# Modulation sets, squares and roots, and low parts of branch weights in a two-layer diffusion trunk

## The chip, the cores and the metric

The kernel runs on one core of one Trainium2 chip. The metric is the device time of one execution in microseconds (us). A core has five engines with their own instruction streams: TensorE (PE, matrix products, written to PSUM), VectorE (DVE), ScalarE (ACT), GpSimd (POOL) and SyncE (SP), which issues the loads and stores. SBUF is the working memory, and PSUM holds eight banks of 512 float32 columns. An engine waits on semaphores that other engines or transfers raise, and works its own list strictly in order.

## The reference, cut to what matters

Two sequences go through two layers with the same weights: 512 latent tokens and 128 context tokens. The kernel keeps them side by side as 640 columns.

```python
def trunk_layer(x, cvec, lp, mix_fn):
    sh1, sc1, g1, sh2, sc2, g2 = modulation(cvec, lp['w_mod'], lp['b_mod'])
    mixed, kv = mix_fn(rmsnorm(x, lp['norm1_g']) * (1.0 + sc1) + sh1)
    x = x + g1 * mixed
    x = x + g2 * swiglu(rmsnorm(x, lp['norm2_g']) * (1.0 + sc2) + sh2, lp['w_ffn_in'], lp['w_ffn_out'])
    return x, kv

def merge_branches(out_a, out_b, out_c, gates, lp, lam_init):
    ...
    ga, gb, gc = jnp.split(jax.nn.sigmoid(gates), N_BRANCH, axis=-1)
    return (ga * ya + gb * yb + gc * yc) @ lp['w_out']

def modulation(cvec, w_mod, b_mod):
    m = jax.nn.silu(cvec) @ w_mod + b_mod
    return [t[:, None, :] for t in jnp.split(m, N_MOD, axis=-1)]

def rmsnorm(x, g):
    y = xf * lax.rsqrt(jnp.mean(xf * xf, axis=-1, keepdims=True) + EPS)
    return (y * g.astype(jnp.float32)).astype(x.dtype)
```

`D_MODEL` is 1024, the FFN is 2816 wide, and everything is float32. After the second layer there is one more `rmsnorm`.

## The kernel before

**Products.** Activations lie as eight tiles of 128 channels by 640 tokens. A product in float32 is made of three in a faster format: weight and activation are each split into a high part and a low part, and `group` (L486) issues high x high (L491), high x low (L492) and low x high (L493) over a half of 320 tokens. Weights come in chunks of 128x1024, 512 KB each, through `weights` (L386): SP loads `raw` (two buffers), ACT copies it to `whi`, rounding it, and the low part `wlo` is raw minus whi. There are four buffers of each. The low part is made in one of two ways. Normally POOL subtracts (`ptt`, L375). For chunks with the flag `add`, which are the input projection, the gates and the branch projections from the tenth chunk on, ACT writes minus raw, rounded, into `wlo`, and POOL issues a transfer that adds raw to it in the DMA engines (`dma_add`, L380). After L0's branch C come the chunks of the output projection, and they are POOL's again.

**A layer.** Attention with its three branches; then `gate_tile` (L1460) for branch C, the merge: for each of eight channel tiles a gate product (one chunk) and a branch product (half a chunk), tanh on ACT, and on DVE `th` times the branch, added to `acc` and split into `u`. Then `out_proj` (L1523): eight tiles times two halves of tokens, 24 matmuls each; DVE adds the residual (`residual`, L1515) from the bank, ACT squares the result (`square_add`, L702), DVE adds the square to `ssq`, and the bank was given back before the square. `rstd` (L712) sums `ssq` over the channels with a product by ones (L717), and ACT and DVE make the reciprocal root; `norm` (L731) then makes the high and low parts of h per tile: DVE multiplies x by a column and by the root, ACT adds the shift, and DVE, or POOL for tiles 2 and 5, makes the low part. Then the FFN in three parts of 8, 8 and 6 tiles (`PARTS`): `ffn_in`, whose tiles from the fourth on use seven half products in place of eight (`seven`, L1638), with sums of weights made on DVE into `ws` and `raw2` (`sums` in `weights`), and sums of h made on DVE into `act` and `ht` (`seven_inputs`, L1607); then `ffn_out` (L1729), whose last part ends with the residual, the squares and the next norm.

**Modulation.** A layer has 24 sets of 256 outputs: sets 0 to 7 for shift and scale of norm 1, 8 to 11 the first gate, 12 to 19 shift and scale of norm 2, 20 to 23 the second gate. They are computed on DVE while PE works (`mod_dve`, L565): SP loads a 128x512 piece `mr` of the transposed weight (four buffers), DVE multiplies it by the vector of one of the two sequences and sums the row (L617). A set takes eight such instructions, and then a few of 128x4 (`mod_finish`, L683). The vectors lie in the PSUM tiles named S at a merge and in banks named B (tag T) in an FFN. Layer 0's sets 0 to 7 are done at the start; its sets 8 to 19 during layer 0's merge and `out_proj`; its sets 20 to 23 and layer 1's sets 0 to 19 during layer 0's FFN; and layer 1's sets 20 to 23 during layer 1's FFN.

**What sets the order.** Every engine's list is fixed when the program is built. `_Order` is a small planner: tasks (generators) with priorities offer their next instruction to an engine with an assumed cost, and the engine takes the one that is ready with the lowest number. Dense products have 1000, modulation 200, the norms about 8. Four PSUM banks are shared by the tags D (up to four) and T (up to two), four more hold the scores S and later the tag F; the FFN uses six of them in turn.

Of the kernel before, what the change touches and what calls it, by code (L numbers as in the profile page):

```python
# [27 lines left out]
ALU = mybir.AluOpType  # L28
# [54 lines left out]
MOD_SOON, MOD_SPREAD = 0.7, 0.75  # L83

ADD_FROM = 10
ENGINES = ("PE", "ACT", "DVE", "POOL", "SP")

# [170 lines left out]
class _Trunk:  # L258
# [127 lines left out]
    def weights(self, plan):  # L386
# [6 lines left out]
        for i, (l, src) in enumerate(plan):  # L393
            seven = isinstance(src, tuple)
            n = 4 if seven else 1
            c = {"l": l, "src": src, "seven": seven, "add": i >= ADD_FROM and not seven and src < O_WO, "hi_ok": [self.ev() for _ in range(n)],
                 "lo_ok": [self.ev() for _ in range(n)]}
            for e in ("loaded", "loaded2", "s1", "s3", "s4"):
                c[e] = self.ev()
            todo.append(c)  # L400
# [164 lines left out]
    def mod_dve(self, steps, prio, each, home):  # L565
# [5 lines left out]
        sets = list(dict.fromkeys(s for _, ss in steps for s in ss))  # L571
        left = {s: 4 for s in sets}
        n = 512 if home == "T" else D
# [32 lines left out]
        def use():  # L606
            md = yield from self.get("md", [P, 512])
            ma = (yield from self.get("ma", [P, 8 * len(sets)])).rearrange("p (j q c s) -> p j q c s", q=2, c=2, s=2)
            for at, pieces, ok, done in plan:
                yield self.wait(ok)  # L610
                for (l, j), q, i, e, d in pieces:
                    a = ma[:, sets.index((l, j))]
                    yield self.wait(e)
                    for c in range(2):
                        o = 0 if at is not None else i * 512
                        b, r = cv[c][:, o:o + 512], a[:, q, c, i:i + 1]
                        yield ("DVE", each, lambda w=d["raw"], b=b, r=r: nc.vector.scalar_tensor_tensor(  # L617
                            md, w, 1.0, b, op0=ALU.mult, op1=ALU.mult, accum_out=r), 0.13)
                    self.rel("mr")
                    left[l, j] -= 1  # L620
                    if left[l, j] == 0:
                        yield self.tt(a[:, :, :, 0], a[:, :, :, 0], a[:, :, :, 1], ALU.add)
                        yield from self.mod_finish(l, j, a[:, :, :, 0])
                self.o.fire(done)
            for t in ("ma", "md", home, home):
                self.rel(t)
# [55 lines left out]

    def mod_finish(self, l, j, t):  # L683

        out = self.modc[l][:, 2 * j:2 * j + 2, :]
        bm = self.small[l][:, S_BM + 2 * j:S_BM + 2 * j + 2].rearrange("p (q o) -> p q o", o=1).to_broadcast([P, 2, 2])
        yield self.tt(out, t, bm, ALU.add)
        which = j // 4
        if which in (1, 4):
            k = 2 * (j % 4)  # L690
            g = (S_N1 if which == 1 else S_N2) + k
            a = self.acol[l][:, 8 * (which == 4) + k:8 * (which == 4) + k + 2, :]
            gb = self.small[l][:, g:g + 2].rearrange("p (q o) -> p q o", o=1).to_broadcast([P, 2, 2])
            yield self.stt(a, out, 1.0, gb, ALU.add, ALU.mult)
        elif which == 2:
            k = 2 * (j % 4)
            yield self.ts(self.g1h[l][:, k:k + 2, :], out, 0.5, None, ALU.mult)
        self.o.fire(self.mod_ok[l][j])

    def square_add(self, x, half, ssq, first):  # L702
        s = slice(half * HALF, (half + 1) * HALF)
        if first:
            yield self.act(ssq, x[:, s], AF.Square)
        else:
            q = yield from self.get("sq", [P, HALF])
            yield self.act(q, x[:, s], AF.Square)
            yield self.tt(ssq, ssq, q, ALU.add)
            self.rel("sq")  # L710

    def rstd(self, ssq):  # L712

# [15 lines left out]
        return ssq  # L729

    def norm(self, l, which, x, half, ssq, h, ready, done):  # L731

        r = yield from self.rstd(ssq)
        left = [KT]

        def one(kt):
# [26 lines left out]
            if left[0] == 0:  # L763
                self.rel("ssq")
                self.o.fire(done)

# [756 lines left out]
    def out_proj(self, l, order, x2, ssq, ssq_ok):  # L1523
# [16 lines left out]
        for m, half in order:  # L1540
# [188 lines left out]
    def ffn_out(self, l, part, act, act_ok, x, ssq, ssq_ok, save):  # L1729
# [6 lines left out]
        def after(m, half, d):  # L1736
            yield self.wait(self.mod_ok[l][20 + m // 2])
            xh = x[m][:, half * HALF:(half + 1) * HALF]
            yield from self.residual(x[m], xh, d, half, self.modc[l][:, 40 + m, :])
            self.bank_done(d)  # L1740
            if not end:
                return
            if m == half == 0:
                self.o.spawn(self.preload(), 8)
            yield from self.square_add(x[m], half, ssq[half], m == 0)
            hits[half]()
# [35 lines left out]
    def layer(self, l, h, norm1, close):  # L1782
# [79 lines left out]
        def control():  # L1862
# [25 lines left out]
            yield self.wait(out_done)  # L1888
            if l == 0:
                for j in range(8, 20):  # L1890
                    yield self.wait(self.mod_ok[l][j])
                mctx.close()
            octx.close()
# [7 lines left out]
            no.close()  # L1901
            mctx = self.pool("m", mods)
            here, ahead = [(l, j) for j in range(20, 24)], [(l + 1, j) for j in range(20)]
            steps = [((0,), here), ((1,), here)]
            if not last:
                steps += [((1,), ahead), ((0,), ahead)]
            self.mod_dve(steps, 200, MOD_SPREAD, "T")
            for i in range(2):
# [5 lines left out]
            else:  # L1914
                done = self.ev()
                h = self.norm_both(l + 1, 0, x2, ssq3, ssq3_ok, done)
                for j in range(20):
                    yield self.wait(self.mod_ok[l + 1][j])
            yield self.wait(ffn_done)
            mctx.close()  # L1920
            fctx.close()
# [311 lines left out]
```

## Time and profile before

| | |
|---|---|
| three runs, median (lowest to highest) | 2412.13 us (2408.89 to 2419.16) |
| the profiled execution's own time | 2411.09 us |
| its span, first to last instruction | 2409.3 us |
| mean granted clock of PE | 0.983 of 2.4 GHz |
| busy: PE, DVE, ACT, POOL | 96%, 74%, 53%, 38% |
| instructions | 44479 |

The page's times are microseconds unless marked ns, L12 is line 12 of the code, an idle time is put down to whatever released the engine last, and names of tiles stand as out<-in without their numbers. PE's matmuls overlap each other: a stretch in which PE is busy all the time can still run at one of two clocks.

### The profile page before, as it was taken

Reading aid. Unit: us, or ns where it says so; the run is one execution under the profiler, and the core shown is the slowest. Engines: PE = TensorE matmul, PEld = TensorE weight load, DVE = VectorE, ACT = ScalarE, POOL = GpSimd, SP = SyncE. Lnnn points to the kernel's source line nnn. Section 1 sums busy time; section 2 is a strip of 40 time slices with the busy share of each in tenths; the row PEclk is TensorE's granted clock in tenths of the full one; section 3 lists DMA queues with packets and bytes.
Section 4 is the critical chain, followed back from the end, with each engine's and each line's share of the span. In section 5 each row is a group of like instructions: output and inputs, shape, how many; then the busy total and the mean of one; then the engine's idle time right before and its main releaser. Section 6 shows DMA issues by size and latency. Waiting matters only on the chain.

```text
span 2409.3 us, 44479 instructions
## 1 busy us (share of the span) xinstructions
PE 2314.3 (96%) x16628; PEld 2265.0 (94%) x16628; DVE 1771.2 (74%) x4151; ACT 1273.9 (53%) x2818; POOL 914.1 (38%) x770
## 2 busy tenths in 40 slices
PE   7999899999998999999999999999999999999997
PEld 4999899999998999999889998999999989999997
DVE  7577788668489998999765778887672499666375
ACT  5677677667434432422457776777664254234143
POOL 3533411322123454645523425112221335456372
PEclk9999999999999999999989999999999999999998
DMA  6234332433774355453245444224436423322222
GB/s 252 75 94 115 77 85 59 108 88 88 207 233 151 107 164 172 135 171 128 95 135 123 99 111 98 72 64 101 107 85 145 133 100 114 106 71 85 74 76 74
DMA packets 100583, 275.79 MB, mean 114 GB/s; under 512 B 11408, under 2 KB 25360, under 8 KB 100368
## 3 DMA queue, kind: packets, MB, share of 16 engines
q1 hardware_dynamic: 84528, 215.28, 26.9%
q0 software_dynamic: 15840, 57.68, 12.5%
q8 instruction: 131, 2.15, 0.4%
q14 instruction: 84, 0.69, 0.1%
HBM read 208.43 MB, written 6.82 MB: 89 GB/s over the span
## 4 chain that ended last, share of the span: by engine, by line
PE 63%; DVE 13%; issue 7%; POOL 4%; DMA 3%; ACT 3%; DVEq 0%; POOLq 0%; SPq 0%; ACTq 0%
PE B L491 9%; PE B L492 8%; PE B L493 8%; PE F L493 6%; PE F L492 6%; PE F L491 5%; PE B L1127 4%; PE B L821 2%; PE B L823 2%; PE B L822 2%; PE S L1099 2%; POOL wlo L375 2%; PE S L1098 2%; PE B L1363 2%; PE B L1362 2%
## 5 line engine op out<-in xcount | busy, mean ns | idle before, releaser
L375 POOL TENSOR_TENSOR wlo<-raw,whi 128x1024 fp32r<-128x1024 f32 x158 | 391.9, 2486 | 350.5 <-ACT whi L336 340.4
L336 ACT ACTIVATE whi<-raw 128x1024 fp32r<-128x1024 f32 x268 | 282.9, 1055 | 257.7 <-PE F L492 89.7
L491 PE MATMUL B<-h,whi 128*128 128x320 f32 x972 | 308.2, 317 | 0.3 <-DVE acc L363 0.3
L493 PE MATMUL B<-h,wlo 128*128 128x320 f32 x972 | 301.0, 310 | 0.2 <-DMA wlo<-raw 0.2
L492 PE MATMUL B<-h,whi 128*128 128x320 f32 x972 | 300.6, 309 | 0.0
L821 PE MATMUL B<-whi,h 128*128 128x256 f32 x928 | 276.0, 297 | 1.8 <-ACT nat L336 1.2
L823 PE MATMUL B<-whi,h 128*128 128x256 f32 x928 | 264.6, 285 | 2.8 <-POOL h L375 2.5
L822 PE MATMUL B<-wlo,h 128*128 128x256 f32 x928 | 264.0, 284 | 0.0
L382 POOL DMA_DIRECT2D wlo<-raw x110 | 98.9, 899 | 323.9 <-ACT wlo L336 78.9
L336 ACT ACTIVATE P<-S,mx 128x768 f32<-128x768 f32 (+4 forms) x240 | 180.9, 756 | 54.6 <-DVE mx L1112 42.2
L491 PE MATMUL B<-u,whi 128*128 128x320 f32 x640 | 202.2, 316 | 0.4 <-DVE u L363 0.4
L375 POOL TENSOR_TENSOR wlo<-ws,whi 128x1024 fp32r<-128x1024 f32 x76 | 143.0, 1881 | 156.8 <-ACT whi L336 147.8
L493 PE MATMUL B<-u,wlo 128*128 128x320 f32 x640 | 198.3, 310 | 4.2 <-DMA wlo<-raw 4.2
L1112 DVE TENSOR_REDUCE mx<-S 128x1 f32<-128x768 f32 (+4 forms) x240 | 182.0, 765 | 22.7 <-PE S L1099 20.1
L492 PE MATMUL B<-u,whi 128*128 128x320 f32 x640 | 198.0, 309 | 0.0
L491 PEld LDWEIGHTS B<-h,whi 128*128 128x128 f32 x972 | 183.3, 189 | 1.3 <-DVE acc L363 0.6
L493 PEld LDWEIGHTS B<-h,wlo 128*128 128x128 f32 x972 | 182.9, 188 | 0.7 <-DMA wlo<-raw 0.7
L492 PEld LDWEIGHTS B<-h,whi 128*128 128x128 f32 x972 | 183.4, 189 | 0.0
L823 PEld LDWEIGHTS B<-whi,h 128*128 128x128 f32 x928 | 178.7, 193 | 3.9 <-POOL h L375 3.1
L821 PEld LDWEIGHTS B<-whi,h 128*128 128x128 f32 x928 | 179.0, 193 | 3.3 <-ACT nat L336 1.9
L822 PEld LDWEIGHTS B<-wlo,h 128*128 128x128 f32 x928 | 179.5, 193 | 0.0
L359 DVE TENSOR_TENSOR PT<-B,PT 128x512 fp32r<-128x512 f32 (+2 forms) x264 | 155.1, 608 | 32.5 <-ACT PT L336 30.5
(212 smaller groups left out, 7338.7 us busy)
## 6 DMA issues: line engine op xcount, KB each, us to landing
raw<-w SPq DMA_DIRECT2D x268, 512.0 KB, 3.4
wlo<-raw POOLq DMA_DIRECT2D x110, 512.0 KB, 4.7
mr<-wt SPq DMA_DIRECT2D x160, 256.0 KB, 3.2
u<-wm SPq DMA_DIRECT2D x12, 512.0 KB, 8.9
cr<-cb SPq DMA_DIRECT2D x14, 256.0 KB, 4.5
x<-x SPq DMA_DIRECT2D x8, 320.0 KB, 7.5
xr<-x SPq DMA_DIRECT2D x16, 160.0 KB, 3.5
xm<-x SPq DMA_DIRECT2D x8, 320.0 KB, 4.2
```

The costliest lines, as they stand in the source:

```text
L336: fn = lambda: self.nc.scalar.activation(out, in_, func, **kw)
L359: return self.dve(_n(out), lambda: self.nc.vector.tensor_tensor(out, a, b, op=op))
L375: return ("POOL", 0.147 + 0.0021 * _n(out), lambda: self.nc.gpsimd.tensor_tensor(out, a, b, op=op), 0.08)
L382: return ("POOL", 1.0, lambda: self.nc.gpsimd.dma_start(out=out, in_=in_, accum_op=ALU.add), 4.5)
L491: mm(out, lhsT=wh, rhs=xh, start=first, stop=False)
L492: mm(out, lhsT=wh, rhs=xl, start=False, stop=False)
L493: mm(out, lhsT=wl, rhs=xh, start=False, stop=last)
L821: mm(d, lhsT=hh, rhs=wh, start=kt == 0, stop=False)
L822: mm(d, lhsT=hh, rhs=wl, start=False, stop=False)
L823: mm(d, lhsT=hl, rhs=wh, start=False, stop=kt == KT - 1)
L1112: yield self.dve(w, lambda: nc.vector.tensor_reduce(m, s[:, 0:w], axis=AX.X, op=ALU.max, negate=True))
L1127: nc.tensor.transpose(t[:, i * P:(i + 1) * P], a, self.ident)
```

## The change

1. `MOD_AHEAD = 12`: layer 0's FFN computes layer 1's sets 0 to 11 only; layer 1's sets 12 to 23 go to layer 1's merge and `out_proj`, with the same code as layer 0's sets 8 to 19, and layer 1's FFN has no modulation left.
2. Four sets end together: the sum of their two halves, the bias and the scale are one instruction of 128x16 in place of four of 128x4.
3. In `out_proj` and in the last part of `ffn_out`, the square is written into the PSUM bank that held the product (`bank`), and the bank is given back after the sum. In the norms but the first, the reciprocal root goes to the bank of the product by ones (`stay`), which is held until the norm's half is done.
4. `NO_ADD`: the last four gates and the last two branch chunks of branch C, in both layers, get their low parts by POOL's subtraction.

```diff
+MOD_AHEAD = 12
+
+NO_ADD = (*range(O_G + 20, O_G + 24), O_BR + 10, O_BR + 11)
...
-            c = {"l": l, "src": src, "seven": seven, "add": i >= ADD_FROM and not seven and src < O_WO, "hi_ok": [self.ev() for _ in range(n)],
+            c = {"l": l, "src": src, "seven": seven, "add": i >= ADD_FROM and not seven and src < O_WO and src not in NO_ADD, "hi_ok": [self.ev() for _ in range(n)],
...
-        left = {s: 4 for s in sets}
+        left = {(l, j // 4): 16 for l, j in sets}
...
-                    left[l, j] -= 1
-                    if left[l, j] == 0:
+                    left[l, j // 4] -= 1
+                    if left[l, j // 4] == 0:
+                        s = sets.index((l, j // 4 * 4))
+                        a = ma[:, s:s + 4].rearrange("p j q c s -> p (j q) c s")
                         yield self.tt(a[:, :, :, 0], a[:, :, :, 0], a[:, :, :, 1], ALU.add)
-                        yield from self.mod_finish(l, j, a[:, :, :, 0])
+                        yield from self.mod_finish(l, j // 4 * 4, a[:, :, :, 0], 4)
...
+        elif bank is not None:
+            yield self.act(bank, x[:, s], AF.Square)
+            yield self.tt(ssq, ssq, bank, ALU.add)
...
-        self.rel("D")
+        if not stay:
+            self.rel("D")
...
-        yield self.stt(ssq, u, 1.5, ssq, ALU.add, ALU.mult)
+        r = d if stay else ssq
+        yield self.stt(r, u, 1.5, ssq, ALU.add, ALU.mult)
...
-        r = yield from self.rstd(ssq)
+        stay = l > 0 or which > 0
+        r = yield from self.rstd(ssq, stay)
...
-                self.rel("D")
                 self.rel("xr")
                 if first_ and half == 0:
                     self.o.spawn(self.preload(), 8)
-                yield from self.square_add(x2[m], half, ssq[half], first_)
+                yield from self.square_add(x2[m], half, ssq[half], first_, d)
+                self.rel("D")
...
-            if l == 0:
-                mctx = self.pool("m", mods)
-                self.mod_dve([((0, 1), [(l, j) for j in range(8, 20)])], 200, MOD_SOON, "S")
+            late = range(8, 20) if l == 0 else range(MOD_AHEAD, 24)
+            mctx = self.pool("m", mods)
+            self.mod_dve([((0, 1), [(l, j) for j in late])], 200, MOD_SOON, "S")
...
-            here, ahead = [(l, j) for j in range(20, 24)], [(l + 1, j) for j in range(20)]
...
+                here, ahead = [(l, j) for j in range(20, 24)], [(l + 1, j) for j in range(MOD_AHEAD)]
+                self.mod_dve([((0,), here), ((1,), here + ahead), ((0,), ahead)], 200, MOD_SPREAD, "T")
```

What moves in the lists. On PE only the two products by ones of layer 0's second norm change place, by six and by nine matmuls. Three places on other engines follow; lines are those of each program.

POOL's list at layer 0's merge, from the last addition of branch B on, before:

```order
L375 TENSOR_TENSOR acc_4909<-acc_4909,th_8610 128x320
L382 DMA wlo_8629<-raw_8222 128x1024
L382 DMA wlo_8653<-raw_8516 128x1024
L382 DMA wlo_8737<-raw_8664 128x1024
L382 DMA wlo_8837<-raw_8722 128x1024
L382 DMA wlo_8865<-raw_8798 128x1024
L382 DMA wlo_8965<-raw_8880 128x1024
L382 DMA wlo_9082<-raw_8947 128x1024
L382 DMA wlo_9106<-raw_9018 128x1024
L382 DMA wlo_9206<-raw_9118 128x1024
L382 DMA wlo_9323<-raw_9187 128x1024
L375 TENSOR_TENSOR wlo_9347<-raw_9259,whi_9346 128x1024
```

and now:

```order
L379 TENSOR_TENSOR acc_4909<-acc_4909,th_8610 128x320
L386 DMA wlo_8629<-raw_8222 128x1024
L386 DMA wlo_8653<-raw_8516 128x1024
L386 DMA wlo_8737<-raw_8664 128x1024
L386 DMA wlo_8837<-raw_8722 128x1024
L379 TENSOR_TENSOR wlo_8865<-raw_8798,whi_8864 128x1024
L379 TENSOR_TENSOR wlo_8963<-raw_8880,whi_8962 128x1024
L379 TENSOR_TENSOR wlo_9079<-raw_8944,whi_9078 128x1024
L379 TENSOR_TENSOR wlo_9089<-raw_8999,whi_9088 128x1024
L379 TENSOR_TENSOR wlo_9200<-raw_9104,whi_9199 128x1024
L379 TENSOR_TENSOR wlo_9316<-raw_9135,whi_9315 128x1024
```

Six issues of the adding transfer have become six subtractions; layer 1's list changes in the same way.

DVE's list in the third part of layer 0's FFN, from one chunk's sums of weights (`ws`, `raw`) to the next (`fu`, `fv`, F and B are sums of the seven products, `md` and `ma` a modulation product and its sum, `mo` and `ac` a finished set). Before, the first twelve rows:

```order
L359 TENSOR_TENSOR ws_13943<-ws_13943,raw_13691 128x512
L359 TENSOR_TENSOR act_13786<-F_10259,act_13786 128x320
L359 TENSOR_TENSOR raw_2326_13806<-raw_13691,raw_2326_13806 128x512
L359 TENSOR_TENSOR fu_13968<-B_10262,fv_13947 128x320
L359 TENSOR_TENSOR ma_10485<-ma_10485 128x4
L359 TENSOR_TENSOR F_10260<-F_10260,fv_13947 128x320
L359 TENSOR_TENSOR mo_92<-ma_10485,sm_91 128x4
L359 TENSOR_TENSOR fv_13947<-F_10258,fu_13968 128x320
L617 SCALAR_TENSOR_TENSOR md_10484,ma_10485<-mr_13845,B_10480 128x512
L617 SCALAR_TENSOR_TENSOR md_10484,ma_10485<-mr_13845,B_10481 128x512
L359 TENSOR_TENSOR fu_13968<-B_10263,fu_13968 128x320
L617 SCALAR_TENSOR_TENSOR md_10484,ma_10485<-mr_13876,B_10480 128x512
```

and now the same stretch:

```order
L363 TENSOR_TENSOR ws_13762<-ws_13762,raw_13543 128x512
L363 TENSOR_TENSOR fu_13788<-F_10225,fv_13768 128x320
L363 TENSOR_TENSOR raw_2289_13646<-raw_13543,raw_2289_13646 128x512
L363 TENSOR_TENSOR F_10226<-F_10226,fv_13768 128x320
L363 TENSOR_TENSOR fv_13768<-F_10227,fu_13788 128x320
L363 TENSOR_TENSOR fu_13788<-F_10228,fu_13788 128x320
L363 TENSOR_TENSOR F_10227<-F_10227,fu_13788 128x320
L363 TENSOR_TENSOR B_10229<-B_10229,fv_13768 128x320
L363 TENSOR_TENSOR ws_13762<-raw_13543,ws_13762 128x512
L363 TENSOR_TENSOR F_10227<-F_10227,s_13861 128x320
```

The modulation has left this part: between the sums of weights of its six chunks the list held 45 instructions L617 and now holds none. In the second part the same count, over the seven stretches between its eight chunks, was 17, 13, 7, 6, 6, 6 and 2, and is 17, 6, 7, 6, 5, 6 and 6.

DVE's list at layer 0's second norm, from the sum that takes the channel sums (`nv`) to the first tiles of h, before:

```order
L371 TENSOR_SCALAR nv_10108<-B_10098 128x320
L617 SCALAR_TENSOR_TENSOR md_8590,ma_8591<-mr_10021,S_8587 128x512
L359 TENSOR_TENSOR ssq_8599<-ssq_8599,sq_10122 128x320
L359 TENSOR_TENSOR nu_10107<-ssq_8598 128x320
L359 TENSOR_TENSOR ma_8591<-ma_8591 128x4
L363 SCALAR_TENSOR_TENSOR nu_10107<-nu_10107,nv_10108 128x320
L359 TENSOR_TENSOR mo_88<-ma_8591,sm_87 128x4
L363 SCALAR_TENSOR_TENSOR ssq_8598<-nu_10107,ssq_8598 128x320
L363 SCALAR_TENSOR_TENSOR x_9569<-B_10115,gh_90,xr_10001 128x192
L363 SCALAR_TENSOR_TENSOR x_9569<-B_10115,gh_90,xr_10001 128x128
L363 SCALAR_TENSOR_TENSOR nu_10163<-x_9564,ac_89,ssq_8598 128x320
L363 SCALAR_TENSOR_TENSOR nu_10164<-x_9565,ac_89,ssq_8598 128x320
```

and now:

```order
L375 TENSOR_SCALAR nv_10067<-B_10061 128x320
L367 SCALAR_TENSOR_TENSOR x_9555<-B_10035,gh_90,xr_9937 128x192
L367 SCALAR_TENSOR_TENSOR x_9555<-B_10035,gh_90,xr_9937 128x128
L363 TENSOR_TENSOR nu_10066<-ssq_8598 128x320
L367 SCALAR_TENSOR_TENSOR nu_10066<-nu_10066,nv_10067 128x320
L367 SCALAR_TENSOR_TENSOR B_10061<-nu_10066,ssq_8598 128x320
L363 TENSOR_TENSOR ssq_8599<-ssq_8599,B_10035 128x320
L367 SCALAR_TENSOR_TENSOR nu_10107<-x_9551,ac_89,B_10061 128x320
L367 SCALAR_TENSOR_TENSOR nu_10108<-x_9552,ac_89,B_10061 128x320
```

The modulation's last instructions have gone from between the root's steps to ahead of `nv`, and the square and the root are read from banks B.

## Rows read from the trace of the kernel before

**Rows 1.** The page's first part: busy time, share of the span, instructions.
```profile
PE 2314.3 (96%) x16628; PEld 2265.0 (94%) x16628; DVE 1771.2 (74%) x4151; ACT 1273.9 (53%) x2818; POOL 914.1 (38%) x770
```

**Rows 2.** Waits of PE, whole span: us in total, times, longest us.
```profile
PE B L717 <- DVE ssq L359: 9.4, 5, 3.5
PE F L493 <- POOL wlo L375: 9.2, 7, 1.6
```

**Rows 3.** Busy time by stretch of the span; the first line names the columns.
```profile
core 0: us, PE busy (x) PEld busy (x) DVE busy (x) ACT busy (x) POOL busy (x), PEclk, DMA share, GB/s
650.00:750.00 100.00, 95.05 (x629) 93.58 (x628) 85.53 (x241) 31.55 (x50) 23.44 (x13) 0.98 0.76 227
670.00:692.00 22.00, 18.16 (x114) 17.89 (x113) 14.63 (x42) 6.70 (x12) 4.12 (x3) 0.92 0.78 212
745.00:775.00 30.00, 23.80 (x138) 21.67 (x137) 29.48 (x60) 14.75 (x29) 11.87 (x6) 0.89 0.37 118
810.00:826.00 16.00, 12.09 (x66) 11.60 (x65) 15.97 (x31) 6.91 (x11) 6.74 (x3) 0.79 0.26 83
955.00:1048.00 93.00, 85.64 (x557) 83.03 (x556) 91.32 (x173) 36.10 (x59) 57.59 (x26) 0.98 0.38 124
1128.00:1174.00 46.00, 39.53 (x251) 37.96 (x250) 45.61 (x88) 16.80 (x29) 26.53 (x12) 0.96 0.24 81
1226.00:1248.00 22.00, 16.31 (x79) 14.18 (x78) 19.94 (x50) 16.24 (x35) 5.70 (x6) 0.69 0.60 162
1800.00:1930.00 130.00, 130.00 (x888) 129.92 (x886) 44.56 (x75) 47.73 (x73) 28.87 (x19) 1.00 0.50 134
1940.00:1960.00 20.00, 15.44 (x74) 13.58 (x74) 17.06 (x31) 11.52 (x23) 7.98 (x5) 0.74 0.43 143
1995.00:2010.00 15.00, 9.81 (x50) 9.32 (x49) 14.97 (x30) 6.77 (x11) 6.60 (x3) 0.77 0.32 105
2139.00:2232.00 93.00, 93.00 (x636) 93.00 (x635) 61.78 (x104) 39.46 (x63) 64.70 (x29) 1.00 0.25 86
2293.00:2339.00 46.00, 46.00 (x316) 46.00 (x315) 35.56 (x58) 19.95 (x33) 31.12 (x16) 1.00 0.21 70
2390.00:2409.30 19.30, 4.69 (x25) 3.41 (x23) 14.05 (x26) 5.07 (x10) 3.85 (x4) 0.68 0.38 136
```

**Rows 4.** POOL's timeline in layer 0's merge: start us, us, what, idle before.
```profile
611.82 0.88 POOL L382 DMA_DIRECT2D wlo<-raw  x1
...
682.85 0.86 POOL L382 DMA_DIRECT2D wlo<-raw  x1 [7.53 <-issue]
```

**Rows 5.** Transfers issued from 600 to 705 us: KB each, median us to landing.
```profile
wlo<-raw POOLq DMA_DIRECT2D x11, 512.0 KB, 7.1
```

**Rows 6.** POOL's groups, whole span: busy us, mean ns of one, idle before.
```profile
L375 POOL TENSOR_TENSOR wlo<-raw,whi 128x1024 fp32r<-128x1024 f32 x158 | 391.9, 2486 | 350.5 <-ACT whi L336 340.4
```

**Rows 7.** DVE's timeline at layer 0's second norm.
```profile
747.30 0.49 DVE L359 TENSOR_TENSOR ssq<-ssq,sq 128x320 f32<-128x320 f32 x1
...
750.72 2.28 DVE L359 TENSOR_TENSOR ssq<-ssq,sq 128x320 f32<-128x320 f32 x1
...
753.85 2.37 DVE L359 TENSOR_TENSOR mo<-ma,sm 128x4 f32<-128x4 f32 x1
...
760.43 2.53 DVE L363 SCALAR_TENSOR_TENSOR nu<-x,ac,ssq 128x320 f32<-128x320 f32 x2
...
764.89 3.11 DVE L363 SCALAR_TENSOR_TENSOR nu<-x,ac,ssq 128x320 f32<-128x320 f32 x2
```

**Rows 8.** POOL's timeline at the same norm.
```profile
750.24 2.41 POOL L375 TENSOR_TENSOR wlo<-raw,whi 128x1024 fp32r<-128x1024 f32 x1 [16.04 <-ACT whi L336]
```

**Rows 9.** DVE's groups by shape, whole span: busy us, mean ns, idle before.
```profile
L617 DVE SCALAR_TENSOR_TENSOR md<-mr,B 128x512 f32<-128x512 f32 x224 | 151.8, 678 | 3.4 <-DMA mr<-wt 1.1
...
L363 DVE SCALAR_TENSOR_TENSOR x<-F,mo,x 128x320 f32<-128x320 f32 x30 | 16.5, 550 | 60.9 <-PE F L493 60.9
```

More of the change, by code (lines that the diff above doesn't have):

```diff
@@ L681, in mod_early, with mod_finish, square_add @@
         return [lambda p=p: load(*p) for p in pieces]
[L683 to L687, printed above, removed]
+    def mod_finish(self, l, j, t, sets=1):
+        n = 2 * sets
+        wide = lambda c: self.small[l][:, c:c + n].rearrange("p (q o) -> p q o", o=1).to_broadcast([P, n, 2])
+        out = self.modc[l][:, 2 * j:2 * j + n, :]
+        yield self.tt(out, t, wide(S_BM + 2 * j), ALU.add)
         which = j // 4
+        k = 2 * (j % 4)
         if which in (1, 4):
[L690 to L694, printed above, removed]
+            a = self.acol[l][:, 8 * (which == 4) + k:8 * (which == 4) + k + n, :]
+            yield self.stt(a, out, 1.0, wide((S_N1 if which == 1 else S_N2) + k), ALU.add, ALU.mult)
         elif which == 2:
[L696 to L702, printed above, removed]
+            yield self.ts(self.g1h[l][:, k:k + n, :], out, 0.5, None, ALU.mult)
+        for i in range(j, j + sets):
+            self.o.fire(self.mod_ok[l][i])
+    def square_add(self, x, half, ssq, first, bank=None):
         s = slice(half * HALF, (half + 1) * HALF)
@@ L710, in square_add, with rstd @@
             self.rel("sq")
-    def rstd(self, ssq):
+    def rstd(self, ssq, stay=False):
         nc = self.nc
@@ L725, in rstd @@
         yield self.stt(u, u, -0.5, v, ALU.mult, ALU.mult)
-        yield self.stt(ssq, u, 1.5, ssq, ALU.add, ALU.mult)
+        r = d if stay else ssq
+        yield self.stt(r, u, 1.5, ssq, ALU.add, ALU.mult)
         self.rel("nu")
         self.rel("nv")
-        return ssq
+        return r
     def norm(self, l, which, x, half, ssq, h, ready, done):
-        r = yield from self.rstd(ssq)
+        stay = l > 0 or which > 0
+        r = yield from self.rstd(ssq, stay)
         left = [KT]
@@ L764, in one @@
                 self.rel("ssq")
+                if stay:
+                    self.rel("D")
                 self.o.fire(done)
@@ L1560, in after @@
                     self.o.spawn(self.preload(), 8)
-                yield from self.square_add(x2[m], half, ssq[half], first_)
+                yield from self.square_add(x2[m], half, ssq[half], first_, d)
+                self.rel("D")
                 hits[half]()
@@ L1739, in after @@
             yield from self.residual(x[m], xh, d, half, self.modc[l][:, 40 + m, :])
-            self.bank_done(d)
             if not end:
+                self.bank_done(d)
                 return
@@ L1744, in after @@
                 self.o.spawn(self.preload(), 8)
-            yield from self.square_add(x[m], half, ssq[half], m == 0)
+            yield from self.square_add(x[m], half, ssq[half], m == 0, d)
+            self.bank_done(d)
             hits[half]()
@@ L1888, in control @@
             yield self.wait(out_done)
[L1889 to L1892, printed above, removed]
+            for j in late:
+                yield self.wait(self.mod_ok[l][j])
+            mctx.close()
             octx.close()
@@ L1901, in control @@
             no.close()
-            mctx = self.pool("m", mods)
-            here, ahead = [(l, j) for j in range(20, 24)], [(l + 1, j) for j in range(20)]
-            steps = [((0,), here), ((1,), here)]
             if not last:
-                steps += [((1,), ahead), ((0,), ahead)]
-            self.mod_dve(steps, 200, MOD_SPREAD, "T")
+                mctx = self.pool("m", mods)
+                here, ahead = [(l, j) for j in range(20, 24)], [(l + 1, j) for j in range(MOD_AHEAD)]
+                self.mod_dve([((0,), here), ((1,), here + ahead), ((0,), ahead)], 200, MOD_SPREAD, "T")
             for i in range(2):
@@ L1916, in control @@
                 h = self.norm_both(l + 1, 0, x2, ssq3, ssq3_ok, done)
-                for j in range(20):
+                for j in range(MOD_AHEAD):
                     yield self.wait(self.mod_ok[l + 1][j])
             yield self.wait(ffn_done)
-            mctx.close()
+            if not last:
+                mctx.close()
             fctx.close()
```

## The prediction, made before the change was run

> **What bounds the kernel now.** I read the page's busy shares first: PE works in 96% of the span [rows 1], 2314.3 of 2409.3 us. The change takes no product away, so all that can be won is PE's 95 us of idle time and what it loses at its lower clock. A stretch whose granted clock averages c has lost (1 - c) x its length of work, since the lower level is half of the higher. Then the waits of PE [rows 2]: one kind waits for a squared sum on DVE before the product by ones (9.4 us in 5 waits), another for low parts from POOL in the FFN (9.2 us in 7). The table of stretches [rows 3] says where. Layer 1's merge and its FFN's second and third parts keep PE full at 1.00; layer 0's same three stretches don't, and in its FFN DVE is busy for 91.32 of 93 us and 45.61 of 46 us, against 61.78 and 35.56 in layer 1. There the engine that makes sums of weights and of products also works through modulation sets, and POOL's low part of a sum can't start before the sum. The seams (merge to output projection, the norms, layer 1's entry, the end) make up the rest.
>
> An idle time alone understates a seam: after each one a stretch follows at 1.2 GHz, so I add idle and clock for each.
>
> **The change part by part.** The sum is made against the profiled execution's own 2411.09 us, 1 us below the median of the runs.
>
> *Part 4, low parts of branch C.* In layer 0's merge POOL issues ten adding transfers from 611.82 to 682.85 us, one per (682.85 - 611.82) / 9 = 7.89 us [rows 4]; each lands 7.1 us (median) after its issue [rows 5]. PE takes a chunk's 48 matmuls in 48 x 130 / 888 = 7.0 us, by layer 1's full stretch [rows 3]. So the transfers come slower than PE eats, and by 670 to 692 us the reserve is gone: PE is busy for 18.16 of 22 us at 0.92, so 3.8 idle + 0.08 x 22 = 1.8, 5.6 us lost. A subtraction on POOL takes 2.49 us [rows 6] and POOL is busy for 23.4 of 100 us there [rows 3]. Six of them end some 4.6 us sooner each than six transfers. I take -5; bounds 0 (the loads themselves are late at 227 GB/s) and -5.6. In layer 1 PE has no loss to give back: 0. ACT drops its six copies of minus raw per layer; it is busy for a third of the stretch, so nothing.
>
> *Part 3 at layer 0's second norm* (745 to 775 us). PE is busy for 23.80 of 30 us at 0.89: 6.2 + 3.3 = 9.5 us. DVE is busy for 29.48 of the 30, so its list is the path. Rows of DVE show what holds it [rows 7]: one addition to `ssq` takes 0.49 us, the next 2.28, while POOL's 2.41 us subtraction runs from 750.24 us on [rows 8]; the multiplications by the root, with both inputs in SBUF, take 2.53 and 3.11 us a pair, and a 128x4 instruction of the modulation took 2.37. A shape with one operand in PSUM takes 0.55 us [rows 9], a pair 1.1. With square and root in banks: 2.28 - 0.49 = 1.8, 2.53 - 1.1 = 1.4, 3.11 - 1.1 = 2.0; and the modulation's 2.4 has left the place in the list. Together 7.6 us of DVE. Not all is PE's: the steps between (`nu` times `nu`, the first low parts of h) still have two SBUF inputs and can take over the hold. I take half, -4; bounds 0 and -7.6.
>
> The Trainium skill ("SBUF — State Buffer", "Who interferes with whom") says that a DVE instruction with two SBUF inputs and a GpSimd instruction that reads SBUF exclude each other for a whole instruction, and one with at most one SBUF input is free of it. The trace agrees (2.28 against 0.49 us). The same rule speaks against part 4, which sets twelve POOL readers among DVE's sums; that is the last rival below.
>
> *Part 3 at layer 1's second norm* (1940 to 1960 us): 4.6 idle + 0.26 x 20 = 5.2. It has the same shape, but had no modulation in front and now gets one, placed ahead of the root in the list. I take -3; bounds +2.4 (one more instruction held as in layer 0) and -4.6. Of the two seams' 8.5 us at low clock I take -2 for shorter dips.
>
> *What norm's lead is worth further on.* PE then waits for `ht` at 810 to 826 (3.9 idle) and 1995 to 2010 us (5.2). PE and the DVE chain both arrive earlier: 0; bounds -9.1, both gone, and +4, the norm's lead waited away.
>
> *Part 1, layer 0's FFN, third part* (1128 to 1174 us): 6.5 idle + 0.04 x 46 = 1.8, 8.3 us, where layer 1's twin loses none. The list holds 45 instructions of 678 ns [rows 9] less, 30.5 us of DVE. It becomes like layer 1's: -8; bounds 0 and -8.3.
>
> *Second part* (955 to 1048 us): 7.4 + 1.9 = 9.3 us. Here the count only falls from 57 to 53, but by 7 (4.7 us) in the first two stretches, before PE's gaps. -4; bounds 0 and -9.3.
>
> *Part 1, layer 1's merge* (1800 to 1930 us). 96 instructions of 678 ns are 65 us of DVE, which has 130 - 44.6 = 85 free; their 48 pieces of 256 KB are 12.6 MB, 97 GB/s on top of 134, as in layer 0's merge (227). PE is full there, and layer 0's merge carries such a load with a loss only where the adding transfers ran dry. +1 for small collisions; bounds 0 and +6.7, that loss and the greater part of one hold (5.6 + 1.1). What leaves layer 1's FFN had cover: PE is full there, so 0.
>
> *Part 2* saves a few instructions of 128x4 among 4151: 0 by itself, since they stand beside PE's full stretches; bounds 0 and -2.4, one held one.
>
> *Part 3 at layer 1's entry* (1226 to 1248 us): 5.7 idle + 0.31 x 22 = 6.8. The root's two banks are now held until a norm's half is done while the first products look for banks: squares unheld against banks late, -0.5; bounds -5.7 and +5.6 (two held pairs as in [rows 7], 2.53 + 3.11, before a bank comes free). *End* (2390 to 2409.3 us): one unheld sum or so, -0.7; bounds 0 and -1.8.
>
> Sum: -5 - 4 - 3 - 2 + 0 - 8 - 4 + 1 - 0.5 - 0.7 = -26.2. **2411.1 - 26.2 = 2385 us.**
>
> **Rivals.**
> *R1, POOL is late in layer 0's FFN, not DVE.* PE's wait names POOL, busy for 57.6 of 93 us. Then the FFN's 12 us stay: 2397. Against it: POOL is busier still, 64.7, in layer 1, where PE doesn't wait.
> *R2, the banks shorten nothing* (the change doesn't do what it says): POOL's holds move to the next DVE instruction with two SBUF inputs. The norms' -9 stay: 2394. For it: the instruction held is whichever meets POOL, and POOL's work is the same.
> *R1 and R2 together*: 2406.
> *R3, layer 1's merge now repeats layer 0's loss*: DVE at 85% and loads at 227 GB/s make PE wait as layer 0's did, +5.6 in place of +1, and the queue runs on into layer 1's second norm, whose -3 and half of the -2 for dips don't come, with one more held instruction of 2.4. 2385 + 4.6 + 4 + 2.4 = 2396. Against it: those waits lay on the transfers that the change removes.
> *The slower one: POOL's new subtractions hold DVE in the merges.* DVE's sums there (`acc` plus `th`) read two SBUF operands, and each can meet a subtraction of 2.41 us [rows 8]. Six per layer are 14.5 us, and DVE has 100 - 85.5 = 14.5 us free in layer 0's merge [rows 3]: it decides from the point at which all six fall on such a sum and the slack is used up by the products' own waits. Then 2 x 14.5 = 29 on PE's path, and the gains of merge and norms (-14) don't come; those of the FFN, entry and end (-8 - 4 - 0.5 - 0.7 = -13.2) do: 2411.1 + 29 - 13.2 = 2427. Against it: DVE has few such sums per chunk, and POOL's 2.5 us come once in 7.0.
>
> **How the numbers follow.** A measurement of this kernel can tell about 0.5%, 12 us, from no change. Forecast 0.54 (its own range 2374 to 2396, the larger bounds not all on one side); R1 0.12, of it 0.09 faster by more than that and 0.03 within; R2 0.12, faster; R1 with R2 0.06, within; R3 0.10, lying near the edge, of it 0.06 faster and 0.04 within; the slower one 0.06. Faster 0.54 + 0.09 + 0.12 + 0.06 = 0.81, the same 0.03 + 0.06 + 0.04 = 0.13, slower 0.06. The range leaves out the last, R1 with R2, and the tails: 2373 to 2403.
>
> **What would show it.** Right: PE has no row of idle time at 670 to 692 us; the FFN's wait for POOL's low parts falls from 9.2 to some 3 us; layer 0's third part shows PE full and DVE near 36 of 46 us; every addition to `ssq` at the norms takes 0.49 us; layer 1's merge keeps PE at 130 of 130. Wrong: `nu` times `nu` or the low parts of h show 2 to 3 us at the norms while PE waits as before (R2); PE still waits in the second and third parts with DVE idle (R1); PE idle in layer 1's merge (R3); `acc` plus `th` at 2 to 3 us beside POOL's subtractions (the slower one).

## The result, and the profile after

The changed kernel takes **2375.8 us** (median; 2372.8 to 2376.78) against 2413.4 us for the kernel before: a ratio of 0.984, 95% interval 0.9825 to 0.9855. A second set of runs gave 0.9847 (0.9834 to 0.9861). The profiled execution took 2376.15 us, 34.9 less than the one of before. The forecast was 26 us less, 2385 us, with a range of 2373 to 2403: right in sign and inside the range, 9 us too careful.

The page's first part, to be laid beside [rows 1]:

```profile
PE 2296.5 (97%) x16628; PEld 2253.8 (95%) x16628; DVE 1724.6 (73%) x4076; ACT 1261.5 (53%) x2807; POOL 933.0 (39%) x770
```

PE's busy time fell by 17.8 us for the same 16628 products, and its idle time from 2409.3 - 2314.3 = 95.0 to 2374.4 - 2296.5 = 77.9 us, by 17.1. So **about half of the gain is waiting and half is clock**: the mean granted clock rose from 0.983 to 0.992, by which the low clock cost an estimated 0.017 x 2409 = 41 us before and 0.008 x 2374 = 19 us now. The 22 us between them, from two rounded means, are enough for the 17.8. A wait that goes can take the slow stretch behind it along.

The waits of PE, as in [rows 2]:

```profile
PE F L497 <- POOL wlo L379: 6.5, 5, 1.3
PE B L726 <- DVE ssq L363: 5.7, 4, 2.9
...
PE B L497 <- POOL wlo L379: 2.3, 2, 1.3
```

The wait for the product by ones fell from 9.4 to 5.7, the FFN's for POOL's low parts in banks F only from 9.2 to 6.5, where the prediction had named some 3 as its sign; in banks B they fell from 3.9 to 2.3. Where they are, the table of stretches shows (columns as in [rows 3]; each stretch is moved forward by what the kernel had gained up to it):

```profile
650.00:750.00 100.00, 100.00 (x683) 99.84 (x682) 91.49 (x239) 33.48 (x56) 34.66 (x15) 1.00 0.60 198
...
738.00:768.00 30.00, 28.41 (x185) 27.02 (x184) 25.79 (x59) 20.04 (x43) 13.10 (x9) 1.00 0.37 120
...
940.00:1033.00 93.00, 86.79 (x575) 83.92 (x574) 92.67 (x194) 36.54 (x62) 59.90 (x27) 1.00 0.38 128
1100.00:1146.00 46.00, 46.00 (x316) 46.00 (x315) 35.96 (x55) 19.41 (x32) 32.69 (x16) 1.00 0.21 73
1199.00:1221.00 22.00, 16.91 (x90) 15.16 (x89) 20.18 (x54) 17.15 (x40) 5.83 (x9) 0.77 0.61 159
1772.00:1902.00 130.00, 129.60 (x884) 129.34 (x883) 103.47 (x274) 43.81 (x72) 38.77 (x19) 1.00 0.70 214
1912.00:1932.00 20.00, 18.41 (x119) 17.17 (x117) 17.86 (x46) 15.38 (x36) 10.00 (x9) 1.00 0.25 80
...
1985.00:2025.00 40.00, 36.34 (x245) 35.55 (x244) 31.97 (x46) 16.40 (x28) 24.86 (x12) 1.00 0.19 65
```

Layer 0's merge, its FFN's third part and both second norms are nearly full now, at full clock. The second part still idles for 6.2 us (DVE 92.67 of 93), and layer 1's FFN, which before had only two waits of 0.5 us in its first part behind those for `ht`, now idles for 3.7 us at 1985 to 2025.

Since both programs issue the same number of products in almost the same order, the k-th product's start in one trace can be set against the k-th in the other. The growth of the difference over a stretch is what the stretch won; below, "by product" means this reading:

| stretch | forecast, us | measured, us |
|---|---|---|
| layer 0's merge | -5 | -6.9 |
| its second norm, with half of the -2 for clock | -5 | -6.9 |
| `ht` and FFN's first part | 0 | -0.7 |
| FFN's second part | -4 | -2.4 |
| FFN's third part | -8 | -9.7 |
| layer 1's entry | -0.5 | -1.1 |
| layer 1's merge | +1 | +0.7 |
| its second norm, with half of the -2 | -4 | -6.4 |
| `ht` and its FFN | 0 | -3.1 + 2.7 |
| end | -0.7 | -0.9 |

Outside these stretches the start gave 0.9 us, the attentions took 0.3 and what follows the last product took 0.4. Every stretch, with `ht` and the FFN of layer 1 taken together, came out within 2.4 us of its forecast. Whether the parts named for them earned it, only experiments can tell.

### The profile page after: what moved, and what is told of

Read it like the earlier page. It is cut to its first block, busy times and chain, and to the rows that moved or that the text cites. A ratio compares the mean times of both kernels' runs of the same rounds, so it can differ in the third digit from the quotient of the medians.

```text
span 2374.4 us, 44401 instructions
## 1 busy us (share of the span) xinstructions
PE 2296.5 (97%) x16628; PEld 2253.8 (95%) x16628; DVE 1724.6 (73%) x4076; ACT 1261.5 (53%) x2807; POOL 933.0 (39%) x770
## 4 chain that ended last, share of the span: by engine, by line
PE 73%; DVE 9%; issue 4%; POOL 2%; ACT 2%; DMA 1%; DVEq 0%; POOLq 0%; ACTq 0%
PE B L495 10%; PE B L497 10%; PE B L496 10%; PE F L497 7%; PE F L496 7%; PE F L495 7%; PE B L1141 4%; PE B L835 3%; PE B L837 3%; PE B L836 3%; PE S L1113 2%; PE S L1112 2%; PE B L1377 2%; PE B L1376 2%; DVE act L363 2%
## 5 line engine op out<-in xcount | busy, mean ns | idle before, releaser
L379 POOL TENSOR_TENSOR wlo<-raw,whi 128x1024 fp32r<-128x1024 f32 x170 | 423.3, 2497 | 402.5 <-ACT whi L340 395.2
L495 PE MATMUL B<-h,whi 128*128 128x320 f32 x944 | 299.1, 317 | 0.3 <-DVE acc L367 0.3
L497 PE MATMUL B<-h,wlo 128*128 128x320 f32 x944 | 291.9, 309 | 0.4 <-DMA wlo<-raw 0.4
L496 PE MATMUL B<-h,whi 128*128 128x320 f32 x944 | 291.5, 309 | 0.0
L386 POOL DMA_DIRECT2D wlo<-raw x98 | 88.5, 903 | 245.9 <-ACT wlo L340 62.0
L495 PEld LDWEIGHTS B<-h,whi 128*128 128x128 f32 x944 | 177.6, 188 | 1.3 <-ACT acc L340 0.6
L497 PEld LDWEIGHTS B<-h,wlo 128*128 128x128 f32 x944 | 177.2, 188 | 1.0 <-DMA wlo<-raw 1.0
L496 PEld LDWEIGHTS B<-h,whi 128*128 128x128 f32 x944 | 177.7, 188 | 0.0
```

The costliest lines, as they stand in the source:

```text
L379: return ("POOL", 0.147 + 0.0021 * _n(out), lambda: self.nc.gpsimd.tensor_tensor(out, a, b, op=op), 0.08)
L386: return ("POOL", 1.0, lambda: self.nc.gpsimd.dma_start(out=out, in_=in_, accum_op=ALU.add), 4.5)
L495: mm(out, lhsT=wh, rhs=xh, start=first, stop=False)
L496: mm(out, lhsT=wh, rhs=xl, start=False, stop=False)
L497: mm(out, lhsT=wl, rhs=xh, start=False, stop=last)
```

## The experiments

**Each part undone in the changed kernel.** The kernel before took 2415.0 us beside the four runs that follow. *Part 4:*

```diff
-NO_ADD = (*range(O_G + 20, O_G + 24), O_BR + 10, O_BR + 11)
+NO_ADD = ()
```

> The changed kernel with NO_ADD empty: the last six low parts of branch C come from the adding transfers again, in both layers; all else as changed. My theory (the transfers, one per 7.9 us, ran dry in layer 0's merge; matched by product, the changed kernel won 6.6 us between 650 and 692 us): the gap of 3.8 us and the clock dip come back in layer 0, some 2382 us, and up to 6 us more if layer 1's merge, now with twelve sets, repeats it (2388). Rival (the merge was late by its loads or by DVE, and gained because the list around it moved): at most 2378 us, no wait of PE for a transferred low part.

It took 2397.1 us, ratio 0.9923 (0.9908 to 0.9938): 21 us of loss, beyond even the larger case expected. By product, 11.5 us are lost between 600 and 745 us, and 9.6 us more than in the changed kernel in layer 1's merge. The wait of PE for a transferred low part:

```profile
PE B L497 <- DMA wlo<-raw: 11.6, 5, 3.1
```

and the stretches of this kernel in layer 0's and in layer 1's merge:

```profile
650.00:700.00 50.00, 44.99 (x276) 44.46 (x275) 34.19 (x98) 15.13 (x24) 6.76 (x6) 0.90 0.83 224
1800.00:1850.00 50.00, 47.19 (x310) 46.71 (x309) 33.32 (x96) 20.29 (x32) 5.24 (x6) 0.97 0.82 219
```

The transfers run dry, and in layer 1 as soon as twelve sets are loaded beside them. Part 1 needs part 4: that is my R3, and part 4 is what keeps it away.

*Part 3:* the squares go through `sq`, the bank is given back ahead of them, and `stay = False`.

> The changed kernel with squares, and reciprocal roots, in SBUF as before; all else as changed. Matched by product, the second norms won 7.2 us in layer 0 and 6.4 us in layer 1. My theory (a DVE instruction with two SBUF operands waits for the end of a POOL subtraction that has begun, and PSUM operands free the sums and the multiplications of this): most of it goes again, 2384 to 2389 us, and additions to ssq or multiplications by the root show 1.5 to 2.5 us holds. Rival (the holds only move to nu times nu and the low parts of h, as two of them in the changed profile did, 2.69 and 2.74 us; what was won came from the modulation's leaving the place between the root's steps): at most 2379 us.

2389.9 us, ratio 0.9898 (0.9881 to 0.9914): 14 us, the theory's side. By product the two second norms lose 6.2 and 6.4 us, nearly all that they had won, so neither the modulation's leaving nor the order made it.

*Part 1:*

```diff
-MOD_AHEAD = 12
+MOD_AHEAD = 20
```

> The changed kernel with MOD_AHEAD = 20: layer 0's FFN again carries layer 1's sets 0 to 19, and layer 1's merge only sets 20 to 23; all else as changed. My theory (DVE is the late engine in layer 0's FFN): the second and third parts lose their 12 us again, PE waits for low parts with DVE over 95% busy, layer 1's merge wins back 0.7: 2386 to 2389 us. Rival (POOL is the late engine and the sets are hidden, the 12 us came from other instructions around): 2375 to 2378 us.

2378.4 us, ratio 0.9848 (0.9833 to 0.9862): no difference that can be told from the changed kernel. The theory falls, as far as it makes the sets DVE's load. Layer 0's third part carries its sets again and is still nearly full; by product it loses 2.2 us to the changed kernel, of which layer 1's entry gives 0.8 back:

```profile
1100.00:1146.00 46.00, 45.63 (x312) 45.37 (x311) 42.89 (x68) 17.96 (x30) 31.38 (x15) 1.00 0.21 74
```

So something other than the sets' departure freed most of it. *And part 1 driven further*, `MOD_AHEAD = 8`:

> The changed kernel with MOD_AHEAD = 8: four more sets move from layer 0's FFN to layer 1's merge and output projection; all else as changed. The second part of layer 0's FFN still has four waits of PE for low parts, 5.1 us. My theory (DVE's load makes them): they go or halve, and layer 1's merge takes 16 sets, 128 instructions of 0.68 us, 87 us of DVE where 85 were free, so that some 2 us are lost there: 2371 to 2376 us. Rival (these waits are a hold of the sums of weights by POOL's two subtractions in a row, as in layer 1's first part, where no set is left and three such waits stand): they stay, and layer 1's merge or its norm loses 3 to 8 us: 2378 to 2384 us.

2397.7 us, ratio 0.9928 (0.9913 to 0.9943). It is worse than either expected: the second part does win some 3 us more, but three of its four waits stay at 1.3 to 1.4 us (the fourth falls to 0.5), and behind layer 1's merge one wait takes it all back:

```profile
PE F L495 <- DVE md L621: 27.0, 1, 27.0
PE B L726 <- DVE ssq L363: 12.7, 4, 7.3
```

128 instructions of 0.68 us don't fit into the free DVE time, the rest runs past the merge, and the FFN's bank F isn't there until the sets have given up S.

**What freed layer 0's FFN.** What `MOD_AHEAD = 20` shares with the changed kernel, and before lacks, is part 2. So before with part 2 alone (`mod_dve` and `mod_finish` of the change):

> The kernel before with part 2 of the change alone: sets end by fours. With layer 0's FFN loaded with twenty sets again, its third part kept 7 to 8 us of the gain, so the count of sets is not what it hung on. Theory A (each set's end has small instructions with two SBUF operands, and each can wait some 2.4 us for a POOL subtraction; by fours there are a quarter of them): most of the FFN's 12 us comes with this part alone, and perhaps 2 us of the second norm, whose held 128x4 instruction goes: ratio to before 0.993 to 0.996, some 2399 to 2406 us. Theory B (the FFN's gain needs the other parts, the earlier arrival after the norm above all): 0.998 to 1.000.

2401.5 us, ratio 0.9947 (0.9929 to 0.9965): **12.5 us** from an edit that I had costed at nothing. By product the FFN's last two parts win 10.3 us. Its third part, beside [rows 3], has 40.2 in place of 45.6 us of DVE:

```profile
1128.00:1174.00 46.00, 44.30 (x301) 43.77 (x300) 40.19 (x61) 19.71 (x34) 28.91 (x15) 1.00 0.20 70
```

DVE's set ends in layer 0's FFN by shape (busy us, mean ns of one, idle before), in this kernel:

```profile
L359 DVE TENSOR_TENSOR ma<-ma 128x16 f32<-128x16 f32 x6 | 8.7, 1457 | 0.1
...
L359 DVE TENSOR_TENSOR mo<-ma,sm 128x16 f32<-128x16 f32 x6 | 1.0, 172 | 0.1
```

and in the kernel before:

```profile
L359 DVE TENSOR_TENSOR ma<-ma 128x4 f32<-128x4 f32 x24 | 19.2, 801 | 0.5
L359 DVE TENSOR_TENSOR mo<-ma,sm 128x4 f32<-128x4 f32 x24 | 12.2, 507 | 0.5
```

An instruction on four columns costs 0.15 us when nothing is in its way (the shortest of these) and up to 2.36 us when POOL is subtracting. The trace of before shows the hold directly: 16 of the 48 took more than 0.3 us, and each of these 16 ended 0.02 us behind the end of a POOL instruction that had begun ahead of it. 24 sets spent 31.4 us on the 48, 24 us of it held; by fours it is 9.7 us. These holds, and not the 0.68 us products, made the difference between a full DVE and one with slack in the third part. The converse, sets ended singly in the changed kernel:

```diff
-        left = {(l, j // 4): 16 for l, j in sets}
+        left = {s: 4 for s in sets}
...
-                        yield from self.mod_finish(l, j // 4 * 4, a[:, :, :, 0], 4)
+                        yield from self.mod_finish(l, j, a[:, :, :, 0])
```

> The changed kernel with sets ended one by one again, twelve ahead as changed. Layer 0's third part has no set left, so it keeps its gain. Theory A (set ends are held by POOL): the second part loses 2 to 5 us and layer 1's merge, with twelve set ends, perhaps 1 to 3: 2378 to 2383 us. Theory B (set ends matter nowhere): 2375 to 2377 us.

2387.6 us, ratio 0.989 (0.9874 to 0.9906): 12 us lost, in theory A's direction and more than it said. By product, 11 us of it lie in the second part; the third, without sets, keeps its gain.

**Which half of part 3.** Squares alone back in SBUF, then roots alone:

In `out_proj`, and likewise in `ffn_out`:

```diff
+                self.rel("D")
-                yield from self.square_add(x2[m], half, ssq[half], first_, d)
-                self.rel("D")
+                yield from self.square_add(x2[m], half, ssq[half], first_)
```

> The changed kernel with the squares in SBUF and the roots in PSUM. Both back in SBUF cost 13 us. Theory A (a norm has one or two held additions of squares ahead of its root, and five or six held multiplications, so the roots carry the larger part): 2 to 5 us lost, 2378 to 2381 us. Theory B (the held addition lies ahead of the product by ones, where PE waits, and counts fully, while multiplications have other halves to do meanwhile): 8 to 13 us lost, 2384 to 2389 us.

```diff
-        stay = l > 0 or which > 0
+        stay = False
```

> The changed kernel with the roots in SBUF and the squares in PSUM, the other half of the pair. Theory A (the roots carry the larger part): 8 to 11 us lost, 2384 to 2387 us. Theory B (the squares carry it): 0 to 5 us lost, 2376 to 2381 us.

2387.9 us (0.989, 0.9874 to 0.9906) and 2385.9 us (0.988, 0.9863 to 0.9898): 12 and 10 us, which together are far more than the 14 of both. In the profiled executions 1.7 us of each lie ahead of the norms, where these edits change nothing. By product the squares alone lose 13.6 us at the two second norms, as much as both halves undone (12.6), and the roots alone 7.6. So theory B is right on the squares and neither is right on the pair: the halves don't add up. Leaving the squares in SBUF is enough to lose all that part 3 wins at the norms; that one held instruction on the path does it, I read from the rows below, no run separates it. DVE at layer 0's second norm, with squares in SBUF:

```profile
749.67 2.05 DVE L363 TENSOR_TENSOR ssq<-ssq,sq 128x320 f32<-128x320 f32 x1
...
760.74 2.39 DVE L363 TENSOR_TENSOR ssq<-ssq,sq 128x320 f32<-128x320 f32 x1 [0.43 <-ACT sq L340]
```

with roots in SBUF:

```profile
748.78 3.16 DVE L367 SCALAR_TENSOR_TENSOR nu<-x,ac,ssq 128x320 f32<-128x320 f32 x2
...
753.77 3.61 DVE L367 SCALAR_TENSOR_TENSOR nu<-x,ac,ssq 128x320 f32<-128x320 f32 x3
```

and with both in PSUM, the changed kernel:

```profile
737.50 0.49 DVE L363 TENSOR_TENSOR ssq<-ssq,B 128x320 f32<-128x320 f32 x1 [0.51 <-ACT B L340]
...
741.60 2.69 DVE L367 SCALAR_TENSOR_TENSOR nu<-nu,nv 128x320 f32<-128x320 f32 x1
...
745.13 1.00 DVE L367 SCALAR_TENSOR_TENSOR nu<-x,ac,B 128x320 f32<-128x320 f32 x2
...
748.41 2.74 DVE L367 SCALAR_TENSOR_TENSOR h<-nu,mo,h 128x320 fp32r<-128x320 f32 x2
```

Two holds remain there, on `nu` times the root's term and on a low part of h, as R2 said they would; but two in place of the three or four of these runs and of before leave PE idle for 1.6 us of the stretch in place of 6.2. The operand in the bank is what frees an instruction: in the kernel before, all ten additions of a square that began while POOL was at work took 1.09 to 2.45 us; in the changed kernel 14 additions from a bank B began so, and none took more than 0.49.

**The new waits in layer 1's first part.** DVE's timeline there, in the changed kernel:

```profile
1995.42 2.89 DVE L363 TENSOR_TENSOR ws<-raw 128x512 f32<-128x512 f32 x1 [0.41 <-POOL wlo L379]
...
1998.64 2.49 DVE L363 TENSOR_TENSOR ws<-ws,raw 128x512 f32<-128x512 f32 x1
```

and POOL's:

```profile
1995.36 5.22 POOL L379 TENSOR_TENSOR wlo<-raw,whi 128x1024 fp32r<-128x1024 f32 x2
```

The two engines have fallen into step: POOL's release of the one buffer `ws` starts its next two subtractions and lets DVE begin the two sums, the first of them 0.06 us after POOL, and they are held for 2.9 and 2.5 us. Before, only the first was held in this part, since POOL's second subtraction came later. DVE there, in the kernel before:

```profile
2028.82 2.89 DVE L359 TENSOR_TENSOR ws<-raw 128x512 f32<-128x512 f32 x1 [0.34 <-POOL wlo L375]
...
2032.03 0.68 DVE L359 TENSOR_TENSOR ws<-ws,raw 128x512 f32<-128x512 f32 x1
```

and POOL:

```profile
2028.76 2.41 POOL L375 TENSOR_TENSOR wlo<-raw,whi 128x1024 fp32r<-128x1024 f32 x1
2033.35 2.63 POOL L375 TENSOR_TENSOR wlo<-raw,whi 128x1024 fp32r<-128x1024 f32 x1 [2.19 <-ACT whi L336]
```

POOL waited 2.19 us for ACT's rounding copy `whi`, and the second sum slipped into the pause. In this chunk a copy of a modulation vector, which waited 2.04 us for its load, stood ahead of `whi` in ACT's list; such copies have left with the sets. A second `ws` should break the step:

```diff
-            fctx = self.pool("f", {"act": SEG, "s": 2, "ht": 8, "raw2": 2, "ws": 1, "fu": 1, "fv": 1})
+            fctx = self.pool("f", {"act": SEG, "s": 2, "ht": 8, "raw2": 2, "ws": 2, "fu": 1, "fv": 1})
...
-                mctx = self.pool("m", mods)
+                mctx = self.pool("m", {**mods, "mr": 3})
```

It ran with the changed kernel itself beside it, and with a third in which part 1 is undone as well.

> The changed kernel itself, beside the next two on the same chip: some 2376 us.

> The changed kernel with two buffers ws in place of one in the FFN, and three in place of four buffers mr there to make room, so that a chunk's first sums of weights stand earlier in DVE's list than the last use of the chunk before. In the changed kernel PE waits four times in layer 0's second part (5.1 us) and three times in layer 1's first part (3.7 us) for a low part of ws; each time the two sums before it were held for 2.9 and 2.5 us by two subtractions of POOL in a row. My theory (the one buffer ties the sums to the moment at which POOL starts these two): most of the 8.8 us go, 2367 to 2371 us. Rival (POOL's own list is what is late, or the holds come along with the sums): 2374 to 2378 us, the waits stand.

> The same with MOD_AHEAD = 20, part 1 of the change undone. The changed kernel lost some 2 us with 20 sets ahead, no more than a measurement can tell. Theory A (part 1 is worth nothing by itself: the sets have room beside the sums once they end by fours): within 3 us of the kernel with two buffers. Theory B (part 1 is masked in the changed kernel by the holds of the sums and pays once these are gone): 5 to 12 us slower than it.

2375.75 (2375.46 to 2376.47), **2369.9** (2367.6 to 2370.3) and **2368.8 us** (2367.4 to 2369.4), ratios 0.9847, 0.9821 (0.9807 to 0.9834) and 0.9816 (0.9803 to 0.9829). Some 6 us of the 8.8 go, and theory A holds for part 1: it is worth nothing that can be measured, masked or not. Both of these beat the changed kernel by little (some 0.25% and 0.3%), but their slowest run, 2370.3, lies under its fastest, 2372.8. The third buffer `mr` went in the same edit and was not tried alone. In layer 0's second part, by shape, the first sum of weights in the changed kernel:

```profile
L363 DVE TENSOR_TENSOR ws<-raw 128x512 f32<-128x512 f32 x5 | 14.2, 2835 | 0.0
```

and with two buffers:

```profile
L363 DVE TENSOR_TENSOR ws<-raw 128x512 f32<-128x512 f32 x5 | 3.4, 680 | 0.0
```

A hold remains in this part, on the third sum (`raw` with `raw`, 2.48 us in place of 0.98 in the mean), where it costs PE less. The two stretches with two buffers, in which 6.2 and 3.7 us had been idle:

```profile
940.00:1033.00 93.00, 90.75 (x614) 89.71 (x613) 91.94 (x205) 38.69 (x63) 63.84 (x29) 1.00 0.40 139
1985.00:2025.00 40.00, 40.00 (x275) 40.00 (x274) 27.18 (x46) 17.62 (x30) 28.04 (x13) 1.00 0.22 72
```

**Part 4 alone**, in the kernel before (`NO_ADD` and its test):

> The kernel before with part 4 of the change alone. Undoing it in the changed kernel cost 21 us, 10 of them in layer 1's merge, which carries twelve sets there; in layer 0's merge the profile showed 12 us where the profiled execution of before lost 6. Theory A (the transfers' loss differs from execution to execution, and the profiled one was a mild case): part 4 alone is worth 7 to 12 us, 2400 to 2406 us, and the runs spread less than before's 8 to 10 us. Theory B (the loss is the 5.6 us of the profile, or less, and the rest of the 21 comes of the changed order around it): 2406 to 2410 us, spread as before.

2403.6 us (2401.2 to 2405.2) against 2413.8 (2409.9 to 2416.1), ratio 0.9958 (0.9945 to 0.9972): 10.3 us, theory A's case. By product its layer 0 merge wins 7.1 us over the profiled execution of before. The profiled execution of before was a fast one, 2.7 us under the median of the runs beside this one. In the profile of part 2 alone, whose merge has the same transfers, the same stretch loses 4.9 us more than before, and with `NO_ADD` empty 4.7 us more. So the transfers' loss is not one number. Whether it differs from execution to execution is not shown: both of these kernels also end their sets by fours in the merge, and that order may cost the transfers more. The spread shrank from 6.1 to 4.0 us, too little to build on.

Parts 4 and 2 alone and part 3 by its undoing make 10.3 + 12.5 + 14 = 37 us of the 37.6. That proves little by itself, since sizes of two kinds are added: undone in the changed kernel, part 4 was worth 21 us. Part 3 was not run alone. That nothing is left for part 1 rests on the two runs with `MOD_AHEAD = 20`.

## Why the prediction was right, and where it was not

- **The place of the gain was right, one cause was wrong.** The step "Part 1, layer 0's FFN, third part ... It becomes like layer 1's: -8", and with it the -4 of the second, sized the stretches well (12 forecast, 12.1 measured) and gave them to the wrong part. With the sets back in place the gain stayed, and with part 2 alone it came. Two stretches that look alike but for one thing don't prove that this thing makes the difference: layer 1's FFN lacked in these parts not only the products but also the set ends. So it is in part luck that the sum came near: the 11 us given to part 1 (-8, -4, +1) were worth nothing, and part 2 with 12.5 and the mis-sized parts 3 and 4 stood in for them.
- **The step "Part 2 saves a few instructions of 128x4 ...: 0 by itself ... bounds 0 and -2.4" failed.** It measured 12.5 us. I counted these instructions by number, and bounded them all by the single one held in [rows 7]. The reason given, "since they stand beside PE's full stretches", doesn't hold: 48 of them stood in layer 0's FFN, in whose last two parts PE idled for 7.4 and 6.5 us. The group by shape had the answer: a mean of 801 ns where the shortest is 0.15 us. The rule that I had cited (the Trainium skill, "SBUF — State Buffer", "Who interferes with whom") has the two engines exclude each other by a lock, and has the order of issue, not the shape, decide who blocks. This trace agrees: 2.36 us for four columns.
- **Part 4** was mis-sized: -5, at most -5.6, where the stretch gave 6.9 and the runs of part 4 alone 10.3. The bound came from one execution's window of 22 us; the loss began before it (by product 1 us was won ahead of 670 us), and it was larger in two other profiles with these transfers.
- **Part 3** was mis-sized by my taking half: the -4 and -3, with -2 for clock, measured 13.3 together. "Can take over the hold" was true of single rows and cost almost nothing.
- **"What leaves layer 1's FFN had cover ... so 0"** was wrong by 2.7 us: what left had kept two engines out of step, by the rows above. The `ht` wait ahead of it gave 3.1, which hid this in the sum.
- **Layer 1's merge**: +1 forecast, 0.7 measured, with DVE at 103 of 130 us; in the second profile of the changed kernel PE loses nothing there. R3 didn't come, and the run without part 4 shows that it would have.
- **R1** is answered by two buffers `ws`: the wait names POOL, but the sums on DVE were late. **The slower rival**'s mechanism is there: `acc` plus `th` rose from 550 to 712 ns and the low parts of `u` from 611 to 853, 16 x (162 + 242) ns = 6.5 us in layer 0, and DVE's busy time from 85.5 to 91.5 us of 100. That is under half of the 14.5 us that would have decided.

## What to carry to other kernels

Where two engines lock each other out, price an instruction by the other engine's, not by its own size: look for small shapes whose mean is several times their minimum, and merge them or move one operand out. When a stretch is explained by comparing it with a twin, list everything that the twin lacks, and try the cheapest item alone first. Where a shared buffer releases both engines at once, a second one lets the short instructions go ahead of the long ones.

## What was not expected of the hardware

Two DVE sums of 0.68 us took 2.9 and 2.5 us chunk after chunk, with nothing else in the way, as long as one release started both engines. Undoing either of two remedies cost nearly as much as undoing both (12, 10 and 14 us; at the two norms 13.6, 7.6 and 12.6). And not every wait costs clock: the second part's waits of 1.26 to 1.34 us in the changed kernel left PEclk at 1.00, while five of 1.08 to 1.56 us there before went with 0.98.
